# Products of 128 columns between longer ones, block sums from kept float32 tiles, and a new order, in a hybrid attention block on one core

## The chip, the core and the metric

The kernel runs on one core of a Trainium2 chip. The core has five engines with a queue each: TensorE (PE in the profile, with its weight loads listed apart as PEld), VectorE (DVE), ScalarE (ACT), GpSimd (POOL) and SyncE (SP), which here only issues DMAs. The metric is the time of one execution on the device, in microseconds (us). The kernel before took 420.25 us (median of three runs, 419.73 to 421.10).

## The reference, cut to what matters

One layer, float32, 512 tokens of 1024 channels. Two attention branches read the same normalised input and are merged by gates:

```python
h = rmsnorm(x, norm_g[l])
(q_lat, c_kv, k_rope, z_a, q_b, k_b, v_b, z_b,
 q_idx, k_idx, w_idx, gate_a, gate_b) = jnp.split(h @ w_in[l], cuts, axis=-1)
# branch a: 8 heads, latent q and k/v, shared rotary key, chunk-causal mask (chunks of 64)
y_a = mla_attention(q_nope, q_pe, k_nope, k_pe, v_a, pos).reshape(B, S, MLA_WIDTH)
y_a = y_a * jax.nn.silu(z_a)
# branch b: 8 heads; an indexer scores the keys, each query keeps its top 128, with a relative bias
y_b = dsa_attention(q_b, k_b, v_b, q_idx, k_idx, w_idx, rel_bias, pos, topk)
y_b = y_b * jax.nn.silu(z_b)
merged = (jax.nn.sigmoid(gate_a) * (y_a @ w_o_a[l])
          + jax.nn.sigmoid(gate_b) * (y_b @ w_o_b[l]))
x = x + merged @ w_out[l]
return rmsnorm(x, final_g)
```

Each branch computes, per head and per tile of 128 queries, `softmax(q @ k.T + mask or bias) @ v`. Because the mask is causal by chunks, query tile i (0 to 3) needs only the first 128 (i + 1) keys.

## The kernel before, in words

**Numbers.** Every float32 operand of a product is kept as two parts, `hi` (rounded for the fast format of TensorE) and `lo` (the rest). A product of two such operands is three products, hi hi, hi lo and lo hi, summed in a PSUM bank (`mm3`); where one operand needs no lo part it is two (`mm`). Every product is one weight load (a block of 128 columns) and one pass of up to 512 columns of the other operand.

**Tiles and room.** Most tiles of 128 x 512 come out of one pool (`slot`) of `NSLOT` = 73 tiles and four that are lent to the rotary tables and the rotary key first. A class of tiles can have a cap (`TCAP` = 5 for temporary tiles, `WCAP` = 8 for split weights). PSUM has 8 banks; the logits (`lg`) may hold two.

**Input.** `normed` makes the normalised input as eight tiles of 128 channels by 512 tokens: a float32 tile `tmp`, from it `hi` and `lo` (`hT[k]`), and gives `tmp` back.

**Projections.** Some are plain (`proj`: 24 products of 512 columns). Others come in pairs of column blocks and use a scheme with seven block products instead of eight (`seven`, called by `proj2` and `values2`, nine groups in all). The scheme needs sums and differences of blocks of the input, `hs`. `input_sums` makes them once `SUMS_AT` is done, which is head 5 of branch a: for each k it adds hi and lo of two input tiles to get float32 back, makes four differences and sums of 256 columns in place, and splits the two results into hi and lo, 16 tiles in all. In `seven`, a bank is taken out by ScalarE or VectorE between some block products, and the next ones that use it wait for that; the fourth product, which comes last, waits for the sum `c22`, an addition on VectorE.

**Heads of branch a** (`mla_head`). For each query tile i in `ORDER` (0, 1, 2, 3), one bank takes three products of 128 (i + 1) columns, lines 1664 to 1666. Then `soft` takes the row maximum on VectorE, the exponential on ScalarE, and normalises.

**Heads of branch b** (`dsa_head`). The mask tile i (16 rounds of top-8 on VectorE made it, `topk`) is copied into a bank by ScalarE, two products of 128 (i + 1) columns are added to it, and `soft` adds the bias on VectorE, then goes on as above.

**Values** (`attend`). The probabilities are turned on TensorE into key-major tiles (`turn`, line 481), split into hi and lo, and multiplied with the values: key tile 0 over 512 query columns, tile 1 over 384, tile 2 over 256, tile 3 over 128, two products each, one after the other in this order. Tile 3's probabilities lie in columns 128 to 256 of the third turned tile.

**Order.** The whole program is one list per engine, written out when the kernel is built. Each piece of work is a generator; a planner (`Flow.run`) keeps a rough clock for each engine and emits, over and over, the step that could start first. `prio` and a tiny random `nudge` (seeded by `DRAW`, and by `REDRAW` once the masks and the rotary key are made) break near ties. `FIRST` names 47 steps of the list at which the second or third candidate on the same engine is taken instead, and `PASSED` four loads of weights that are issued some DMAs later. So a change in any step changes the order of everything behind it. `QUEUE` is the order in which projections are fetched, split and multiplied.

Of the kernel before, what the change touches and what calls it, by code (L numbers as in the profile page):

```python
# [43 lines left out]
REDRAW = 324  # L44
# [121 lines left out]
class Flow:  # L166
# [9 lines left out]
    def __init__(self):  # L176
        self.free = {"PE": 0.6, "ACT": 0.6, "DVE": 0.6, "POOL": 0.6, "SP": 0.6}
        self.hw, self.dma, self.adma = 0.6, 0.0, 0.0
        self.pbias = -1.0
# [3 lines left out]

        self.draw = random.Random(DRAW)

    def spawn(self, gen, prio, nudge=None):
        t = Thread(gen, prio, self.draw.random() * NUDGE if nudge is None else nudge)
        self.threads.append(t)
        self.advance(t, None)
        return t  # L190
# [110 lines left out]
DRAW = 53  # L301
# [6 lines left out]
def tile_block(ctx: ExitStack, tc: tile.TileContext, a: dict, out: bass.AP, bias_dram: bass.AP):  # L308
# [159 lines left out]

    def mm3(ps, w, x, start, stop, more=False):

        return mm(ps, [(w[0], x[0]), (w[0], x[1]), (w[1], x[0])], start, stop, more)
# [102 lines left out]
    mask = [fixed(f"mask{i}", [P, P * (i + 1)]) for i in range(NT)]  # L574
# [68 lines left out]
    xt, eraw, xg, ewq, ewkv, eql, hT = {}, {}, {}, {}, {}, {}, {}  # L643
# [201 lines left out]
    def normed(k):  # L845
        yield Until(lambda: rbc and k in xg)
        tmp = yield slot("tmp", TCAP)
# [6 lines left out]
        put(tmp)  # L854
# [96 lines left out]
    def scores(i):  # L951
# [18 lines left out]
        if score_users[0] == 0:  # L970
            put(*qs.values(), *ks)
        flow.spawn(topk(i), PTOPK)
# [50 lines left out]
    sums_due = [SUMS_AT]  # L1023
# [66 lines left out]
    def input_sums():  # L1090

        yield Until(lambda: sums_due[0] in done)
# [455 lines left out]
    def attend(br, h, probs, ready, prio):  # L1548
# [29 lines left out]
        for kt, pt, src, dst in ((0, 0, slice(0, S), slice(0, S)), (1, 1, slice(P, S), slice(P, S)),  # L1578
                                 (2, 2, slice(256, S), slice(256, S)), (3, 2, slice(P, 256), slice(384, S))):
            hi, lo = turned[pt]  # L1580
            yield mm(ps[:, dst], [(v4[:, kt, :], hi[:, src]), (v4[:, kt, :], lo[:, src])], kt == 0, kt == 3)
            if kt != 2:
                put(hi, lo)
# [52 lines left out]
    def mla_head(h):  # L1636
# [7 lines left out]
        def soft(i, ps):  # L1644
# [3 lines left out]
                mx.tile[:, 1:2], ps.tile[:, :n], op=ALU.max, axis=AX.X, negate=True))], [mx], [ps])  # L1648
            den = yield from sums[i].at(i)
            yield act(probs[i], ps[:, :n], AF.Exp, bias=mx[:, 1:2], scale=1.0, accum=den)  # L1650
            put(ps, mx)
            yield from sums[i].normalise(i, probs[i])
            ready.add(i)

        for i in ORDER:
            nn = P * (i + 1)
            ps = yield bank("lg")

            def emit():
                o = ps.tile[:, :nn]  # L1660
                q0, q1 = qh.tile[:, TOK[i]], ql.tile[:, TOK[i]]
# [664 lines left out]
```

## Time and profile before

| What | Value |
|---|---|
| Runs of the kernel | 419.73, 420.25, 421.10 us |
| Span of the profiled execution | 417.4 us |
| Difference of the median from that span | 2.85 us |
| TensorE busy | 410.4 us, 2494 products, 2494 weight loads |
| VectorE, ScalarE, GpSimd busy | 372.8, 297.9, 125.7 us |
| Granted TensorE clock, 1.00 is full | 1.00 in every window up to 400 us |

The time of the profiled execution itself is not listed beside its span; its span is 2.85 us shorter than the median run, which also holds the program's start and end.

In a row of a group, the line number of the kernel comes first, then engine, operation, output and inputs by tile name (`ps` is a PSUM bank, `s_w` a split weight, `s_hs` a block sum, `s_ph` a turned probability), shapes, and the count; behind the bar, busy us and the mean ns of one, and then the idle time before them with what ended it. Rows of one tile give the shortest, middle and longest duration in ns, and the first and last start. In a row of the timeline the first number is the start and the second the duration, both in us; `x9` means that nine alike are merged, and brackets hold the idle time before with what ended it. A product is recorded from its entry into the array until its result is out, so neighbouring products overlap.

### The profile page before, as it was taken

The numbers are of one execution on the slowest core, as the hardware profiler recorded it, in microseconds if no ns is written. First come the engines' busy times: TensorE is split into PE (matmuls) and PEld (weight loads), VectorE is DVE, ScalarE is ACT, GpSimd is POOL, SyncE is SP. The second block draws the span as 40 slices with busy tenths as digits, with TensorE's granted clock in tenths as the row PEclk, the third lists the DMA queues.
The fourth block names the chain that finished last, engine by engine and source line by source line (L and its number), as shares of the span: only waits on it lengthen the run. The fifth ranks groups of instructions, "written<-read, shape, count | busy, mean of one in ns | idle before, by whom it ended". The sixth has DMA issues, their size and how long they took to land.

```text
span 417.4 us, 7522 instructions
## 1 busy us (share of the span) xinstructions
PE 410.4 (98%) x2494; PEld 370.5 (89%) x2494; DVE 372.8 (89%) x789; ACT 297.9 (71%) x688; POOL 125.7 (30%) x147
## 2 busy tenths in 40 slices
PE   8999999999999999999999999999999999999994
PEld 8999888888888888889999999999998888888883
DVE  4779889569999999999998999799889999999973
ACT  5776888575763846547649978998999975329753
POOL 0037769544464659610000410401001120021330
PEclk9999999999999999999999999999999999999999
DMA  7984135655256351553427336564249767377104
GB/s 266 359 291 143 51 93 190 182 172 136 100 134 188 97 166 40 139 140 110 143 53 204 111 127 175 143 150 149 93 113 296 249 184 240 107 263 264 50 26 176
DMA packets 30790, 65.90 MB, mean 158 GB/s; under 512 B 4792, under 2 KB 6472, under 8 KB 30752
## 3 DMA queue, kind: packets, MB, share of 16 engines
q1 hardware_dynamic: 28400, 61.79, 48.6%
q10 hardware_dynamic: 1584, 2.49, 1.7%
q0 software_dynamic: 768, 1.15, 0.9%
q8 instruction: 19, 0.31, 0.3%
q14 instruction: 19, 0.16, 0.1%
HBM read 50.49 MB, written 4.21 MB: 131 GB/s over the span
## 4 chain that ended last, share of the span: by engine, by line
PE 98%; DVE 0%; ACT 0%; DVEq 0%; issue 0%; ACTq 0%
PE ps L462 88%; PE ps L481 5%; PE ps L1665 1%; PE ps L1666 1%; PE ps L1664 1%; PE ps L957 1%; PE ps L611 1%; DVE s_rg L413 0%; ACT junk L366 0%; PE ps L1008 0%; DVEq L2322 0%; ACT sm L366 0%; DVE sm L2017 0%; DVE zeros L540 0%; DVE neghalf L540 0%
## 5 line engine op out<-in xcount | busy, mean ns | idle before, releaser
L462 PE MATMUL ps<-s_h,s_w 128*128 128x512 f32 (+1 forms) x672 | 135.8, 348 | 0.1
L462 PEld LDWEIGHTS ps<-s_h,s_w 128*128 128x128 f32 x672 | 106.8, 189 | 14.0 <-DVE s_pair L383 0.5
L357 ACT CAST s_w<-raw 128x512 fp32r<-128x512 f32 (+3 forms) x134 | 78.2, 595 | 16.1 <-DVE raw L383 12.1
L385 POOL TENSOR_TENSOR s_w<-raw,s_w 128x512 fp32r<-128x512 f32 (+2 forms) x42 | 52.1, 1253 | 61.5 <-ACT s_w L357 54.1
L383 DVE TENSOR_TENSOR s_w<-raw,s_w 128x512 fp32r<-128x512 f32 (+2 forms) x92 | 59.8, 663 | 9.7 <-ACT s_w L357 9.5
L462 PE MATMUL ps<-s_hs,s_w 128*128 128x256 f32 x384 | 51.9, 285 | 0.0
L462 PEld LDWEIGHTS ps<-s_hs,s_w 128*128 128x128 f32 x384 | 48.3, 191 | 0.1
L462 PE MATMUL ps<-s_ys,s_w 128*128 128x512 f32 x192 | 46.0, 392 | 0.0
L462 PEld LDWEIGHTS ps<-s_ys,s_w 128*128 128x128 f32 x192 | 35.7, 188 | 7.2
L462 PE MATMUL ps<-s_wo,s_mg 128*128 128x512 f32 (+1 forms) x156 | 33.7, 373 | 0.0
L462 PE MATMUL ps<-s_w,s_xg 128*128 128x328 f32 (+1 forms) x192 | 32.5, 323 | 0.0
L462 PEld LDWEIGHTS ps<-s_wo,s_mg 128*128 128x128 f32 x156 | 27.6, 188 | 5.2
L366 ACT ACTIVATE s_p<-s_p,sm 128x256 f32<-128x256 f32 (+3 forms) x58 | 31.0, 548 | 1.4 <-DVE sm L1748 1.3
L462 PEld LDWEIGHTS ps<-s_w,s_xg 128*128 128x128 f32 x192 | 31.4, 188 | 0.0
L357 ACT CAST s_ph<-ps 128x384 fp32r<-128x384 f32 (+1 forms) x48 | 23.6, 517 | 6.7 <-PE ps L481 5.7
L383 DVE TENSOR_TENSOR s_ph<-ps,s_ph 128x384 fp32r<-128x384 f32 (+1 forms) x48 | 27.2, 591 | 1.1 <-ACT s_ph L357 1.1
L366 ACT ACTIVATE s_p<-ps,sm 128x128 f32<-128x128 f32 (+3 forms) x32 | 16.8, 528 | 15.9 <-DVE sm L1647 15.8
L982 DVE MATCH_REPLACE8 mask<-sm,mask 128x384 f32<-128x384 f32 (+2 forms) x48 | 25.9, 542 | 0.0
L981 DVE MAX8 sm<-mask 128x8 f32<-128x384 f32 (+2 forms) x48 | 25.6, 548 | 0.1
L462 PE MATMUL ps<-s_ph,vv 128*128 128x512 f32 (+3 forms) x128 | 25.6, 319 | 0.0
L481 PE MATMUL ps<-ident,s_p 128*128 128x128 f32 x160 | 23.0, 273 | 0.0
L462 PEld LDWEIGHTS ps<-s_ph,vv 128*128 128x128 f32 x128 | 20.6, 189 | 2.0
(206 smaller groups left out, 783.4 us busy)
## 6 DMA issues: line engine op xcount, KB each, us to landing
raw<-w_out SPq DMA_DIRECT2D x18, 512.0 KB, 3.5
s_op<-s_op SPq DMA_DIRECT2D x36, 128.0 KB, 3.4
raw<-w_ga SPq DMA_DIRECT2D x8, 512.0 KB
raw<-w_gb SPq DMA_DIRECT2D x8, 512.0 KB, 3.6
raw<-w_o SPq DMA_DIRECT2D x16, 256.0 KB, 3.6
s_xn<-x SPq DMA_DIRECT2D x8, 256.0 KB, 5.2
bias_scratch<-s_sig ACTq DMA_DIRECT2D x8, 256.0 KB, 2.3
raw<-w_za SPq DMA_DIRECT2D x4, 512.0 KB, 4.5
```

The source lines that it names most:

```text
L357: nc.scalar.copy(dst.ap, src.ap)
L366: nc.scalar.activation(dst.ap, src.ap, func, **kw)
L383: opts.append(("DVE", 0.07 + 0.00104 * x.n, lambda: nc.vector.tensor_tensor(dst.ap, x.ap, y.ap, op=op)))
L385: opts.append(("POOL", 0.15 + 0.0021 * x.n, lambda: nc.gpsimd.tensor_tensor(dst.ap, x.ap, y.ap, op=op)))
L462: nc.tensor.matmul(ps.ap, l.ap, r.ap, start=start and i == 0, stop=stop and i == len(pairs) - 1, skip_group_check=more)
L481: nc.tensor.transpose(d.ap, s.ap, ident.tile)
L611: return lambda: nc.tensor.matmul(ps.tile[:, :n], z[:, :P], z[:, :n], start=True, stop=True)
L957: step = pe(0.005 + n / 2400, [ps.all], [qs[h].all, ks[0].all], lambda: nc.tensor.matmul(ps.tile[:, :n], qs[h].tile[:96, TOK[i]], ks[0].ti ...
L981: yield Step([("DVE", t, lambda: nc.vector.max(m8.tile, work.tile))], [m8], [work])
L982: yield Step([("DVE", t, lambda: nc.vector.match_replace(work.tile, m8.tile, work.tile, MARK))], [work], [m8])
L1664: nc.tensor.matmul(o, q0[0:100], k0[0:100], start=True, stop=False)
L1665: nc.tensor.matmul(o, q0[0:96], k1[0:96], start=False, stop=False)
```

## The change

Three things are changed, and the order is made anew.

1. Short products stand between longer ones. A helper `mixed` emits a list of products that may go to different views of one bank. In the logits, query tiles 2 and 0 share a bank (columns 128 to 512 and 0 to 128), and their products alternate, 384 and 128 columns; tiles 1 and 3 follow alone. In branch b the masks of tiles 0 and 2 lie in one tile of 512 columns and are copied into the shared bank at once. A shared bank is given back when both rows of `soft` are through with it. In `attend` the products of key tile 0 (512 columns) alternate with those of key tile 3 (128 columns) and come first; then come tiles 1 and 2.
2. `normed` keeps its float32 tile (class `hx`, no cap) and `input_sums` works in it, so the additions of hi and lo are gone. The sums start when head 1 of branch a is done.
3. `FIRST` and `PASSED` are empty, `DRAW` is 286 instead of 53 and `REDRAW` 186 instead of 324. `EARLY` and `MOVE` are new names with the old value and an empty table.

The number of products, the weights and the columns of each stay as they are.

```diff
@@ class Flow
-        self.pbias = -1.0
+        self.pbias = EARLY
...
@@
+    def mixed(parts, start, stop, more=False):
+        def emit():
+            for i, (o, l, r) in enumerate(parts):
+                nc.tensor.matmul(o.ap, l.ap, r.ap, start=start and i == 0, stop=stop and i == len(parts) - 1, skip_group_check=True)
...
@@
-    mask = [fixed(f"mask{i}", [P, P * (i + 1)]) for i in range(NT)]
+    two = const.tile([P, 4 * P], F32, name="masks")
+    mask = [Buf(two[:, :P], "mask0"), fixed("mask1", [P, 2 * P]), Buf(two[:, P:], "mask2"), fixed("mask3", [P, 4 * P])]
@@ def normed(k)
-        tmp = yield slot("tmp", TCAP)
+        tmp = yield slot("hx")
...
-        put(tmp)
+        hx[k] = tmp
@@ def input_sums()
-            f = []
-            for i in (k, k + 4):
-                t = yield slot("tmp", TCAP)
-                yield soon(tt(t.all.f, hT[i][0].all.f, hT[i][1].all.f, ALU.add, BOTH))
-                f.append(t)
+            yield Until(lambda: k in hx and k + 4 in hx)
+            f = [hx[k], hx[k + 4]]
@@ def attend
-        for kt, pt, src, dst in ((0, 0, slice(0, S), slice(0, S)), (1, 1, slice(P, S), slice(P, S)),
-                                 (2, 2, slice(256, S), slice(256, S)), (3, 2, slice(P, 256), slice(384, S))):
-            hi, lo = turned[pt]
-            yield mm(ps[:, dst], [(v4[:, kt, :], hi[:, src]), (v4[:, kt, :], lo[:, src])], kt == 0, kt == 3)
+        parts = []
+        for x in range(2):
+            for kt, pt, src, dst in ((0, 0, slice(0, S), slice(0, S)), (3, 2, slice(P, 256), slice(384, S))):
+                parts.append((ps[:, dst], v4[:, kt, :], turned[pt][x][:, src]))
+        yield mixed(parts, True, False)
+        put(*turned[0])
+        for kt, src in ((1, slice(P, S)), (2, slice(256, S))):
+            hi, lo = turned[kt]
+            yield mm(ps[:, src], [(v4[:, kt, :], hi[:, src]), (v4[:, kt, :], lo[:, src])], False, kt == 2, True)
@@ def mla_head
-        for i in ORDER:
+        for tiles in TILES:
             ps = yield bank("lg")
+            tiles = [(i, ps[:, c : c + P * (i + 1)]) for i, c in tiles]
+            yield mixed(logits(0, 0, 100, tiles) + logits(0, 1, 96, tiles) + logits(1, 0, 96, tiles), True, True)
@@ def dsa_head
-        for i in ORDER:
-            ps = yield bank("lg", (0, nn))
-            yield act(ps[:, :nn], mask[i].all)
-            yield mm(ps[:, :nn], [(qb[:, TOK[i]], kh[:, :nn]), (qb[:, TOK[i]], kl[:, :nn])], False, True, True)
+        for tiles in TILES:
+            ps = yield bank("lg", (0, width))
+            if len(tiles) > 1:
+                step = act(ps[:, :width], View(mask[0], two))
...
+            yield mixed([(o, qb[:, TOK[i]], k[:, : P * (i + 1)]) for k in (kh, kl) for i, o in tiles], False, True, True)
@@
-ORDER = [0,1,2,3]
+TILES = (((2, P), (0, 0)), ((1, 0),), ((3, 0),))
+EARLY = -1.0
+MOVE = {}
-FIRST = {
...
-}
-PASSED = {7: 2, 8: 2, 9: 2, 10: 6}
-SUMS_AT = ("a", 5)
+FIRST = {}
+PASSED = {}
+SUMS_AT = ("a", 1)
-REDRAW = 324
+REDRAW = 186
-DRAW = 53
+DRAW = 286
```

More of the change, by code (lines that the diff above doesn't have):

```diff
@@ L184, in __init__ @@
         self.draw = random.Random(DRAW)
+        self.born = {}
     def spawn(self, gen, prio, nudge=None):
-        t = Thread(gen, prio, self.draw.random() * NUDGE if nudge is None else nudge)
+        name = gen.__name__
+        n = self.born[name] = self.born.get(name, 0) + 1
+        drawn = self.draw.random() * NUDGE if nudge is None else nudge
+        t = Thread(gen, prio, MOVE.get((name, n), drawn))
         self.threads.append(t)
@@ L467, in mm @@
         return step
+    def mixed(parts, start, stop, more=False):
+        def emit():
+            for i, (o, l, r) in enumerate(parts):
+                nc.tensor.matmul(o.ap, l.ap, r.ap, start=start and i == 0, stop=stop and i == len(parts) - 1, skip_group_check=True)
+        t = sum(0.0133 + r.n / 2400 for _, _, r in parts)
+        step = pe(t, [o for o, _, _ in parts[:1]], [v for _, l, r in parts for v in (l, r)], emit, len(parts))
+        step.fills = [(o, start and i == 0) for i, (o, _, _) in enumerate(parts)]
+        return step
     def mm3(ps, w, x, start, stop, more=False):
@@ L971, in scores @@
             put(*qs.values(), *ks)
+            done.add("scored")
         flow.spawn(topk(i), PTOPK)
@@ L1642, in mla_head, with soft @@
         ready, sums = set(), sums_of_head()
-        def soft(i, ps):
+        def soft(i, ps, users):
             n = P * (i + 1)
@@ L1742, in dsa_head, with soft @@
         ready, biased, sums = set(), set(), sums_of_head()
[L1744 removed]
+        def soft(i, ps, users):
             n = P * (i + 1)
@@ L1748, in soft @@
             step = Step([("DVE", 0.1 + 0.00104 * n, lambda: nc.vector.tensor_tensor_reduce(
-                p.ap, ps.tile[:, :n], backward(bias.all.f[:, :n]).ap, op0=ALU.add, op1=ALU.min, scale=-1.0, scalar=-FILL,
-                accum_out=mx.tile[:, 1:2]))], [mx, p.buf], [ps, bias])
+                p.ap, ps.ap, backward(bias.all.f[:, :n]).ap, op0=ALU.add, op1=ALU.min, scale=-1.0, scalar=-FILL,
+                accum_out=mx.tile[:, 1:2]))], [mx, p.buf], [ps.buf, bias])
             step.count = 2
             yield step
-            put(ps)
+            users[0] -= 1
+            if not users[0]:
+                put(ps.buf)
             biased.add(i)
@@ L1762, in soft @@
             ready.add(i)
-        for i in ORDER:
-            nn = P * (i + 1)
-            ps = yield bank("lg", (0, nn))
-            yield act(ps[:, :nn], mask[i].all)
-            yield mm(ps[:, :nn], [(qb[:, TOK[i]], kh[:, :nn]), (qb[:, TOK[i]], kl[:, :nn])], False, True, True)
-            spawn(soft(i, ps), prio)
+        for tiles in TILES:
+            width = sum(P * (i + 1) for i, _ in tiles)
+            ps = yield bank("lg", (0, width))
+            if len(tiles) > 1:
+                step = act(ps[:, :width], View(mask[0], two))
+                step.ins.append(mask[2])
+                yield step
+            else:
+                yield act(ps[:, :width], mask[tiles[0][0]].all)
+            tiles = [(i, ps[:, c : c + P * (i + 1)]) for i, c in tiles]
+            yield mixed([(o, qb[:, TOK[i]], k[:, : P * (i + 1)]) for k in (kh, kl) for i, o in tiles], False, True, True)
+            users = [len(tiles)]
+            for i, o in tiles:
+                spawn(soft(i, o, users), prio)
         put(qb, kh, kl)
```

35 lines of the change are left out of this document (14 added, 21 removed), and 4 rows, old and new, of the table FIRST.

## The prediction

> **What bounds the kernel now.** I read the profile's page first: the shares of the engines and the chain that ended last. Then I read the windows by stage, the waits on the weight loads, and single products in order of time.
>
> ```profile
> span 417.4 us, 7522 instructions
> PE 410.4 (98%) x2494; PEld 370.5 (89%) x2494; DVE 372.8 (89%) x789; ACT 297.9 (71%) x688; POOL 125.7 (30%) x147
> ...
> PE 98%; DVE 0%; ACT 0%; DVEq 0%; issue 0%; ACTq 0%
> ```
>
> TensorE is busy for 410.4 of 417.4 us, and the chain lies on it for 98%. The windows (start:end, their length, then busy us and instructions of PE, PEld, DVE, ACT, POOL) say where the other 7.0 us are.
>
> ```profile
> 45.00:110.00 65.00, 65.00 (x350) 55.59 (x349) 53.26 (x102) 46.29 (x110) 38.82 (x49) 1.00 0.52 148
> 110.00:220.00 110.00, 110.00 (x652) 97.53 (x652) 109.09 (x258) 66.20 (x151) 44.49 (x50) 1.00 0.42 116
> 240.00:340.00 100.00, 99.92 (x733) 94.58 (x732) 91.73 (x191) 92.56 (x227) 13.43 (x10) 1.00 0.55 166
> 411.60:417.50 5.90, 0.00 (x0) 0.00 (x0) 1.04 (x3) 1.28 (x4) 0.00 (x0) 0.83 0.49 179
> ```
>
> Most of the idle time, 5.90 us, is the tail behind the last product; between 45 and 340 us TensorE has almost no hole. It has one partner near its limit in each stage: VectorE with 109.09 of 110 us before 220, ScalarE with 92.56 of 100 us after 240. A product is recorded as busy until its result is out, so a short wait does not show as idle on PE. It shows on the weight loads, in brackets with what ended it:
>
> ```profile
> 51.21 0.08 PEld L1008 LDWEIGHTS ps<-s_oh,rbs 64*8 64x8 f32 x1 [0.35 <-issue]
> ...
> 53.07 0.08 PEld L1008 LDWEIGHTS ps<-s_oh,rbs 64*8 64x8 f32 x1 [0.17 <-issue]
> ...
> 260.80 0.76 PEld L462 LDWEIGHTS ps<-s_h,s_w 128*128 128x128 f32 x6 [0.24 <-DVE s_pair L383]
> ...
> 299.81 0.77 PEld L462 LDWEIGHTS ps<-s_h,s_w 128*128 128x128 f32 x6 [0.24 <-DVE s_pair L383]
> ...
> 323.50 0.19 PEld L462 LDWEIGHTS ps<-s_op,qhi 128*128 128x128 f32 x1 [0.44 <-ACT ps L357]
> ```
>
> They add up to 0.35 + 0.17 + 0.24 + 0.24 + 0.44 = 1.44 us. So a better order alone has about 1.4 us to win; a worse one can lose much more. The rest must come from products that take less time each.
>
> **The change part by part.** *Products of 128 columns.* These are the groups that the change puts between longer ones, three in a logits tile of branch a, two in one of branch b, two in the attention values:
>
> ```profile
> L462 PE MATMUL ps<-s_ph,vv 128*128 128x128 f32 x32 | 5.3, 248 | 0.0
> ...
> L462 PE MATMUL ps<-s_op,qhi 128*128 128x128 f32 x16 | 2.7, 258 | 0.0
> ...
> L1666 PE MATMUL ps<-s_op,s_op 96*128 96x128 f32 x8 | 2.2, 276 | 0.0
> L1665 PE MATMUL ps<-s_op,qhi 96*128 96x128 f32 x8 | 2.2, 274 | 0.0
> L1664 PE MATMUL ps<-s_op,qhi 100*128 100x128 f32 x8 | 1.8, 226 | 0.0
> ```
>
> That is 32 + 16 + 24 = 72 products. What one costs is read from a run of three that stands between products of 512 columns, first the loads, then the products, by start time and duration:
>
> ```profile
> 83.24 0.19 PEld L462 LDWEIGHTS ps<-s_h,s_w 128*128 128x128 f32 x1
> 83.47 0.19 PEld L1664 LDWEIGHTS ps<-s_op,qhi 100*128 100x128 f32 x1
> 83.70 0.19 PEld L1665 LDWEIGHTS ps<-s_op,qhi 96*128 96x128 f32 x1
> 83.81 0.19 PEld L1666 LDWEIGHTS ps<-s_op,s_op 96*128 96x128 f32 x1
> 83.92 0.53 PEld L462 LDWEIGHTS ps<-s_h,s_w 128*128 128x128 f32 x3
> 84.50 0.19 PEld L1664 LDWEIGHTS ps<-s_op,qhi 100*128 100x128 f32 x1
> ```
>
> ```profile
> 83.23 0.62 PE L462 MATMUL ps<-s_h,s_w 128*128 128x512 f32 x2
> 83.70 0.23 PE L1664 MATMUL ps<-s_op,qhi 100*128 100x128 f32 x1
> 83.76 0.27 PE L1665 MATMUL ps<-s_op,qhi 96*128 96x128 f32 x1
> ```
>
> Each load starts when the product before it starts: 83.24 against 83.23, 83.70 against 83.70. The load for L1665 is not started at 83.47 or soon after, though the queue had nothing else to load until 83.70: weights are fetched one product ahead and no further. From load to load the run goes 83.70, 83.81, 83.92: 0.11 us for each product of 128 columns. The last of the three is followed by two products of 512 columns, which take (83.70 - 83.23) / 2 = 0.235 us each, up to the load at 84.50: 84.50 - 83.92 - 0.47 = 0.11 us again. The product itself could pass in 0.06 us (83.76 - 83.70: L1665 enters 0.06 us behind L1664, then waits for its weights). What holds it to 0.11 us is the load of the product that comes next, whatever length that has. The first of the run has a long product before it and the last a long one behind it, and both cost 0.11 us like the middle one. Alternated, each short product is first and last at once, and the long product behind it has its weights loaded in the shadow of the short one, as before. So I take 0 us for this part. The bounds: if the loads could run two ahead, 72 x (0.11 - 0.06) = 3.6 us less; nothing makes it dearer, since the count of products and loads stays, 2494 of each.
>
> [...]
>
> *Two logits tiles in one bank.* In branch b the mask copies of 128 and of 384 columns become one of 512.
>
> ```profile
> L357 ACT COPY ps<-mask 128x512 f32<-128x512 f32 x8 | 4.7, 583 | 0.6 <-DVE sm L1748 0.6
> L357 ACT COPY ps<-mask 128x384 f32<-128x384 f32 x8 | 3.8, 476 | 0.0
> ...
> L357 ACT COPY ps<-mask 128x128 f32<-128x128 f32 x8 | 2.1, 276 | 0.0
> ```
>
> ScalarE saves 8 x (0.476 + 0.276 - 0.583) = 1.35 us over the stage from 240 to 340, in which it is busy for 92.56 of 100 us. TensorE is busy for 99.92 us there, so nothing of it reaches the end unless it shortens the 0.44 us wait on ScalarE above. Against it: a head's first product now waits for a copy of 0.583 instead of 0.276 us, 0.31 us later, and the shared bank is free only when both softmax rows have read it. Products of other jobs cover that 0.31 us; without cover it is 8 x 0.31 = 2.5 us. I take 0.
>
> *Block sums from the kept tiles.* The eight additions that rebuilt the float32 input go; the subtractions, casts and low parts stay and come after head 1 of branch a instead of head 5.
>
> ```profile
> L383 DVE TENSOR_TENSOR s_y<-ps,s_tmp x16: 665/689/698, 103.8 to 344.6; 64x512 f32<-64x512 f32 x16
> L394 DVE SCALAR_TENSOR_TENSOR s_tmp<-s_x,normg,s_rbc x8: 740/745/1794, 33.7 to 42.7; 128x512 f32<-128x512 f32 x8
> ...
> L383 DVE TENSOR_TENSOR s_tmp<-s_h,s_h x6: 673/682/684, 172.6 to 186.4; 128x512 f32<-128x512 f32 x6
> ...
> L385 POOL TENSOR_TENSOR s_tmp<-s_h,s_h x2: 1294/1294/1294, 153.9 to 155.1; 128x512 f32<-128x512 f32 x2
> ...
> L357 ACT CAST s_hs<-s_tmp x8: 614/620/645, 159.2 to 190.1; 128x512 fp32r<-128x512 f32 x8
> L383 DVE TENSOR_TENSOR s_hs<-s_tmp,s_hs x7: 670/683/684, 170.6 to 191.3; 128x512 fp32r<-128x512 f32 x7
> ...
> L982 DVE MATCH_REPLACE8 mask<-sm,mask x48: 397/543/682, 100.5 to 215.0; 128x384 f32<-128x384 f32 x16, 128x512 f32<-128x512 f32 x16, 128x256 f32<-128x256 f32 x16
> ```
>
> VectorE loses 6 x 0.682 = 4.1 us and GpSimd 2 x 1.294 = 2.6 us. TensorE had 110.00 of 110 us there, so the gain is 0. The moved rest, 7 x 0.683 = 4.8 us of low parts on VectorE and 8 x 0.620 = 5.0 us of casts on ScalarE among it, falls into the same window; there the search for the top keys (48 replacements, 100.5 to 215.0) is VectorE's work of lowest rank and gives way. Without that cover up to 4.8 us of weight splits would come late; I take 0. The price is room, in a pool of 73 tiles and four lent ones: eight float32 tiles stay from 42.7 us on, when the last is written, and the sixteen sum tiles come up to 50 us earlier, since the first head of branch a ends at 103.8 us and the additions now begin at 153.9.
>
> *The new order.* The hand-written picks (47 steps, four held loads) go, and two new draws break the ties. No row shows what the picks were worth. From below it is the 1.44 us of waits; from above I take the third rival's price. As the pieces that it orders are the same, I take 0, nearer to the rows that show hardly a wait.
>
> **The sum.** 417.4 us of span and 0 + 0 + 0 + 0. The median of the runs, 420.25 us, is 2.85 us above the span of the profiled execution (start and end of the program), and that stays. **Forecast: no change, 420.2 us.** A measurement of this kernel tells about 0.3% from no change, 1.26 us.
>
> **The rivals.** *First, the alternation works*: the load of the long product's weights is hidden after all, because loads are spread over a long and a short product. For it: the first short product's own load is hidden already. Against it: a run of three would then take 0.06 + 0.11 + 0.11 us, and the rows show 0.11 each. Time: 420.2 - 3.6 = 416.6 us. [...]
>
> *Second, the order fills the waits*: the lighter VectorE and ScalarE and the early sums leave none of the 1.44 us. Time: 420.2 - 1.44 = 418.8 us. For it: three of the five waits end on those two engines. Against it: an order without the picks would have to be better everywhere at once.
>
> *Third, slower*: the last of the seven block products of a pair waits for VectorE's addition of the product two before it (the two waits of 0.24 us on s_pair). One product lies between as cover. The code has nine such groups, and their products stand in this row:
>
> ```profile
> L462 PE MATMUL ps<-s_hs,s_w x384: 274/283/365, 194.7 to 314.7; 128*128 128x256 f32 x192
> ```
>
> Seven of the nine show no such wait. In a new order VectorE, busy 91.73 of 100 us there, has other work queued ahead of that addition, or the room for split weights is taken by the sums and heads. Each group stops at three places of the code until ScalarE or VectorE has taken a bank. One wait of 0.24 us per group more is 9 x 0.24 = 2.2 us, 422.4 us; two are 4.3 us. It decides once the addition starts later than the covering product's length, twelve times at most 0.13 us (0.76 / 6 by the row at 260.80), 1.5 us. For it: this stage already has the most waits, and ScalarE has 7 us to spare in 100. Against it: ScalarE and VectorE both lose work.
>
> **How the numbers follow.** No change 0.38; alternation works 0.12, as the rows speak against it plainly; the waits filled 0.18; slower by hand-overs 0.32. The first and second rivals are faster by over 0.3%: 0.30. Slower is 0.32, same 0.38. The range reaches down to the alternation's 416.6 us and up to one and a half waits per group, 420.2 + 3.2 = 423.4 us, rounded outward to 416.5 and 423.6. The forecast's own range is 419.0 to 421.5.
>
> **What would show it.** Alternation: the load behind a 128-column product starts 0.11 us after that product's own start also between 384 or 512 columns (right), or 0.06 to 0.07 us (wrong, first rival). Bank sharing: the mask copies of 128 and 384 columns are gone and ScalarE is some 1.35 us lower. Sums: the group s_tmp<-s_h,s_h is gone and the casts to s_hs start before 130 us instead of at 159.2. Order: the bracketed waits on the weight loads add up to 1.4 us again; over 2.7 us makes the forecast wrong on the slow side. A tail that differs from 5.90 us by over 1 us would also break it.

## The result, and the profile after

The changed kernel takes 423.21 us (median; 422.65 to 424.00) against 420.07 us (419.73 to 421.10) of the kernel before: a ratio of 1.0075, with a 95% interval of 1.0056 to 1.0095. It is 3.1 us slower. The forecast was no change, 420.2 us; the time lies inside the range of 416.5 to 423.6 us.

The page of the profile after, the same lines as before (busy us, share of the span, instructions; then the chain that ended last, by engine):

```profile
span 421.2 us, 7537 instructions
...
PE 411.3 (98%) x2494; PEld 371.1 (88%) x2494; DVE 374.4 (89%) x785; ACT 293.9 (70%) x674; POOL 129.0 (31%) x149
...
PE 44%; DVE 6%; DMA 2%; ACT 2%; issue 1%; DVEq 0%; ACTq 0%
```

The span is 3.8 us longer than the 417.4 us of before, while TensorE works only 0.9 us more. Before, the chain lay on TensorE for 98%. Now it can be followed only from 185.79 us on (the shares add up to 55%), because there it leaves TensorE for VectorE. The windows by stage (start:end, length, then busy us and instructions of PE, PEld, DVE, ACT, POOL, then the granted clock) show which stage lost:

```profile
45.00:110.00 65.00, 64.54 (x348) 55.13 (x347) 55.14 (x104) 45.20 (x106) 39.14 (x48) 1.00 0.51 147
110.00:220.00 110.00, 108.05 (x622) 94.68 (x620) 105.73 (x258) 67.76 (x166) 47.31 (x54) 1.00 0.39 115
240.00:340.00 100.00, 99.47 (x742) 95.25 (x741) 89.56 (x190) 89.81 (x213) 14.53 (x10) 1.00 0.54 160
415.20:421.20 6.00, 0.10 (x1) 0.00 (x0) 1.32 (x4) 1.28 (x4) 0.00 (x0) 0.85 0.48 175
```

TensorE had 110.00 of 110 us before in the second window and has 108.05 now; the first and the third lost about 0.45 us each, and the tail is still 6 us. The waits on the weight loads, in brackets with what ended them, give the places. These are the five longest from 45 us on:

```profile
68.39 0.30 PEld L974 LDWEIGHTS ps<-s_qs,s_qs 96*128 96x128 f32 x2 [0.79 <-DVE s_tmp L387]
...
197.69 1.50 PEld L466 LDWEIGHTS ps<-s_hs,s_w 128*128 128x128 f32 x12 [0.58 <-ACT ps L361]
...
201.60 2.94 PEld L466 LDWEIGHTS ps<-s_hs,s_w 128*128 128x128 f32 x24 [0.97 <-ACT s_pair L361]
205.53 2.93 PEld L466 LDWEIGHTS ps<-s_h,s_w 128*128 128x128 f32 x24 [1.00 <-DVE s_pair L387]
...
327.18 0.30 PEld L478 LDWEIGHTS ps<-s_op,qhi 128*128 128x128 f32 x2 [0.73 <-ACT ps L361]
```

They sum to 0.79 + 0.58 + 0.97 + 1.00 + 0.73 = 4.07 us; four smaller ones, between 52 and 58 us, add 0.78: 4.85 us. Counted alike (every bracket from 45 us on), the kernel before has 1.75 us: the 1.44 of the prediction leaves out two short waits, 0.16 us at 51.45 and 0.15 us at 53.31. That is 3.1 of the 3.8 us. The three in the middle, 2.55 us, lie between 197 and 206 us, in the first of the nine groups of seven block products: its hand-overs from TensorE to ScalarE and VectorE are late. The last of the three, at 205.53, is the wait for the sum `c22`. What VectorE and ScalarE did meanwhile, in the timeline of that stretch (start, duration), a selection:

```profile
191.55 0.55 DVE L999 MAX8 sm<-masks 128x8 f32<-128x384 f32 x1
...
194.04 0.56 DVE L999 MAX8 sm<-masks 128x8 f32<-128x384 f32 x1
194.52 0.67 DVE L387 TENSOR_TENSOR raw<-raw 128x512 f32<-128x512 f32 x1
...
195.23 0.62 ACT L361 CAST s_w<-raw 128x512 fp32r<-128x512 f32 x1 [3.45 <-DVE raw L387]
...
196.75 0.62 ACT L361 CAST s_w<-raw 128x512 fp32r<-128x512 f32 x1 [0.40 <-ACT s_sig L370]
...
197.27 0.37 ACT L361 COPY ps<-ps 128x256 f32<-128x256 f32 x1
...
204.00 0.54 DVE L1000 MATCH_REPLACE8 masks<-sm,masks 128x384 f32<-128x384 f32 x1
204.46 0.68 DVE L387 TENSOR_TENSOR s_w<-s_wsum,s_w 128x512 fp32r<-128x512 f32 x1
205.06 0.42 DVE L387 TENSOR_TENSOR s_pair<-ps,s_pair 128x256 f32<-128x256 f32 x1
```

Read it from the bottom up. The addition that the last block product waits for (205.06, load at 205.53) stands in VectorE's list behind a round of the top-8 search. ScalarE's copy out of the first bank (197.27, load at 197.69) stands behind casts of split weights, and the first of these sat idle for 3.45 us until VectorE had made its operand (194.52), which itself stands behind two rounds of the search and the first step of a third. How much of VectorE's time the search has there, busy us (and instructions) on the mask tiles from 191.5 to 205.5 us, first in the changed kernel:

```profile
191.50:205.50 14.00, 8.34 (x22) 0.00 (x0) 0.00 (x0) 1.00 0.46 152
```

and in the kernel before:

```profile
191.50:205.50 14.00, 1.38 (x5) 0.00 (x0) 0.00 (x0) 1.00 0.42 132
```

8.34 against 1.38 us. The chain of waits from 190 to 212 us, by line, says the same; in the changed kernel TensorE has three tenths of it:

```profile
by line: DVE s_w L387 25.3%; PE ps L466 24.8%; DVE masks L1000 16.6%; DVE sm L999 14.6%; issue 7.3%; DVE raw L387 5.9%; PE ps L478 5.0%; DVE s_pair L387 1.6%; DVEq L387 0.1%
```

while in the kernel before it has all of it:

```profile
by line: PE ps L462 101.0%
```

The parts of the change that can be seen in rows of tiles did happen. The casts to the block sums and the last step of the mask tile of 384 columns, after (first and last start behind the comma):

```profile
L361 ACT CAST s_hs<-s_hx x8: 608/622/630, 118.2 to 154.6; 128x512 fp32r<-128x512 f32 x8
...
L406 DVE TENSOR_SCALAR masks<-masks x1: 350/350/350, 205.4 to 205.4; 128x384 f32<-128x384 f32 x1
```

The sums come 41 us earlier than before (118.2 against 159.2). The search ends at 205.4 us in place of 217.7: it runs earlier, at the cost of what stands beside it.

### The profile page after: what moved, and what is told of

Its sections match the earlier page's. It is cut to its first block, busy times and chain, and to the rows that moved or that the text cites. A ratio compares the mean times of both kernels' runs of the same rounds, so it can differ in the third digit from the quotient of the medians.

```text
span 421.2 us, 7537 instructions
## 1 busy us (share of the span) xinstructions
PE 411.3 (98%) x2494; PEld 371.1 (88%) x2494; DVE 374.4 (89%) x785; ACT 293.9 (70%) x674; POOL 129.0 (31%) x149
## 4 chain that ended last, share of the span: by engine, by line
PE 44%; DVE 6%; DMA 2%; ACT 2%; issue 1%; DVEq 0%; ACTq 0%
PE ps L466 40%; PE ps L478 3%; DVE s_w L387 2%; PE ps L497 2%; DMA raw<-w_zb 1%; DVE masks L1000 1%; DVE sm L999 1%; DMA raw<-w_out 1%; DVE raw L387 0%; ACT s_ys L370 0%; ACT s_w L361 0%; ACT s_p L370 0%; DVE s_y L387 0%; DVE s_wo L387 0%; ACT s_wo L361 0%
## 5 line engine op out<-in xcount | busy, mean ns | idle before, releaser
L387 DVE TENSOR_TENSOR s_w<-raw,s_w 128x512 fp32r<-128x512 f32 (+2 forms) x93 | 61.4, 673 | 8.6 <-ACT s_w L361 8.1
L466 PE MATMUL ps<-s_hs,s_w 128*128 128x256 f32 x384 | 50.6, 284 | 1.1 <-ACT s_pair L361 0.8
L466 PE MATMUL ps<-s_ys,s_w 128*128 128x512 f32 x192 | 44.9, 391 | 0.0
L389 POOL TENSOR_TENSOR s_w<-s_wsum,s_w 128x512 fp32r<-128x512 f32 x3 | 4.3, 1448 | 85.3 <-ACT s_w L361 85.3
L370 ACT ACTIVATE s_p<-s_p,sm 128x384 f32<-128x384 f32 (+3 forms) x52 | 28.3, 564 | 2.2 <-DVE sm L1762 1.8
L478 PE MATMUL ps<-s_op,qhi 128*128 128x256 f32 (+11 forms) x128 | 27.6, 319 | 0.5 <-ACT ps L361 0.5
L478 PEld LDWEIGHTS ps<-s_op,qhi 128*128 128x128 f32 (+2 forms) x128 | 20.9, 189 | 2.8 <-ACT ps L361 0.7
L361 ACT COPY s_tmp<-ps 64x512 f32<-64x512 f32 (+1 forms) x18 | 10.1, 561 | 15.2 <-PE ps L466 12.6
```

Source lines behind the costliest of these rows:

```text
L361: nc.scalar.copy(dst.ap, src.ap)
L370: nc.scalar.activation(dst.ap, src.ap, func, **kw)
L387: opts.append(("DVE", 0.07 + 0.00104 * x.n, lambda: nc.vector.tensor_tensor(dst.ap, x.ap, y.ap, op=op)))
L389: opts.append(("POOL", 0.15 + 0.0021 * x.n, lambda: nc.gpsimd.tensor_tensor(dst.ap, x.ap, y.ap, op=op)))
L466: nc.tensor.matmul(ps.ap, l.ap, r.ap, start=start and i == 0, stop=stop and i == len(pairs) - 1, skip_group_check=more)
L478: nc.tensor.matmul(o.ap, l.ap, r.ap, start=start and i == 0, stop=stop and i == len(parts) - 1, skip_group_check=True)
```

## The experiments

My theory after the result: the parts of the change are worth nothing, and the loss is the new order, at the three hand-overs of the first group, because VectorE's list there holds rounds of the search ahead of the group's work. Rivals: the alternation or the removed additions are worth something by themselves, and the order hides it; the lost picks are the loss; ScalarE or GpSimd is late there, not VectorE; the new structure (shared bank, early sums) cannot be ordered as well.

**Alternation undone, nothing else.** Same plan, but inside one step the short products stand behind the long ones.

```diff
     def mixed(parts, start, stop, more=False):
         def emit():
-            for i, (o, l, r) in enumerate(parts):
+            seen = [(o.first, o.n) for o, _, _ in parts]
+            for i, (o, l, r) in enumerate(sorted(parts, key=lambda p: seen.index((p[0].first, p[0].n)))):
```

> The changed kernel with the alternation alone undone: in the shared banks and in the attention values the short products follow the long ones in one run, on the same plan for all other engines. Theory (a product of 128 columns costs 0.11 us by the next weight load, wherever it stands): the same time as the changed kernel, 423.2 us within 0.5. Rival (alternation hides loads): up to 72 x 0.05 = 3.6 us slower, 426.8 us.

Measured: 422.73 us (422.61 to 423.71) beside 419.93 us of the kernel before; ratio 1.0067 (1.0051 to 1.0082). The alternated kernel has 1.0075, so alternation gains nothing. The loads for two shared logits banks, 12 in all, six of 384 and six of 128 columns, alternated in the changed kernel:

```profile
83.73 0.71 PEld L478 LDWEIGHTS ps<-s_op,qhi 100*128 100x128 f32 x4
84.43 0.30 PEld L478 LDWEIGHTS ps<-s_op,s_op 96*128 96x128 f32 x2
84.72 0.59 PEld L478 LDWEIGHTS ps<-s_op,qhi 100*128 100x128 f32 x4
85.29 0.30 PEld L478 LDWEIGHTS ps<-s_op,s_op 96*128 96x128 f32 x2
85.58 0.53 PEld L466 LDWEIGHTS ps<-s_h,s_w 128*128 128x128 f32 x3
```

and apart, in runs of three:

```profile
83.81 0.42 PEld L479 LDWEIGHTS ps<-s_op,qhi 100*128 100x128 f32 x2
...
84.69 0.19 PEld L479 LDWEIGHTS ps<-s_op,s_op 96*128 96x128 f32 x1
84.80 0.30 PEld L479 LDWEIGHTS ps<-s_op,qhi 100*128 100x128 f32 x2
...
85.67 0.30 PEld L466 LDWEIGHTS ps<-s_h,s_w 128*128 128x128 f32 x2
```

From the first of the 12 to the load behind them: 85.58 - 83.73 = 1.85 us alternated, 85.67 - 83.81 = 1.86 us apart. A short product inside a run takes 84.80 - 84.69 = 0.11 us; an alternated pair of 128 and 384 columns 84.72 - 84.43 = 0.29 us, which is 0.11 and the 0.18 us of a product of 384 columns (loads at 84.23 and 84.41 us, with the products apart).

**The picks alone, and the draws alone.** First the kernel before without its picks.

```diff
-FIRST = {
...
-PASSED = {7: 2, 8: 2, 9: 2, 10: 6}
+FIRST = {}
+PASSED = {}
```

> The kernel before with the hand-written picks and the held loads taken out, its own draws kept. Theory (the loss comes from an order without picks, and not from the new structure): bracketed waits of TensorE and its loads grow from 1.4 to 4 or more us and the time to 422.5 to 426 us. Rival (the early sums and kept tiles cause the loss): 420 to 421 us, hardly a wait more.

Measured: 421.25 us; ratio 1.0029 (1.0019 to 1.0039), less than the 422.5 us that I expected at the least. So the picks were worth 1.3 us on the old structure. Then the same kernel with the new draws on top.

```diff
-REDRAW = 324
+REDRAW = 186
...
-DRAW = 53
+DRAW = 286
```

> The kernel before without picks and with the changed kernel's two draws. Theory (order alone): 422 to 427 us, waits of 3 us or more, at places unlike the changed kernel's. Rival (structure): 420 to 421 us.

Measured: 433.92 us; ratio 1.0325 (1.0306 to 1.0344). Then the changed kernel with the old draws.

```diff
-REDRAW = 186
+REDRAW = 324
...
-DRAW = 286
+DRAW = 53
```

> The changed kernel with the two draws of the kernel before. Theory (order alone): any time from 421 to 427 us, with the waits at other places than 196 to 206 us. Rival (structure: sums early, tiles kept, loads late for the first group of block products): the first group waits again by 2 us or more, 423 us or more.

Measured: 435.81 us; ratio 1.0373 (1.0354 to 1.0392). Both lie above my ranges. Neither pair of draws suits the other structure; each was good only where it stood. Both crossed plans have one long hole near the end. In the waits of the changed kernel with the old draws (us in total, times, longest):

```profile
PEld ps L466 <- DVE s_wo L387: 6.8, 1, 6.8
```

So the other pair of draws costs 433.92 - 421.25 = 12.7 us on the old structure and 435.81 - 423.21 = 12.6 us on the new, four times the effect in question; a single redraw says nothing of a structure.

**Untuned draws on both.** Draws 7 and 7, without picks, on the kernel before and on the changed one, one execution each.

```diff
+REDRAW = 7
...
+DRAW = 7
```

> The kernel before without picks, both draws 7, a number chosen for nothing. Theory (draws that were not selected cost 5 us and more on either structure): 425 to 437 us, with a hole of several us in the output stage near 400 us. Rival (the structure before is the sounder one): under 424 us.

> The changed kernel with both draws 7. Theory (order alone): 425 to 437 us, within 8 us of the kernel before with draws 7 and no picks. Rival (the new structure costs time by itself): slower than that one by 3 us or more.

Measured: 442.83 us on the old structure, 426.51 us on the new. They differ by 16.3 us, twice what I allowed. That does not show the new structure to be better, since each is one plan out of many. The totals give no support to the rival that it can't be ordered as well; what stands in the first group does, as the table further down shows.

**The additions removed, on the old plan.** The planner reckons with the eight additions, but they are not emitted.

```diff
-                yield soon(tt(t.all.f, hT[i][0].all.f, hT[i][1].all.f, ALU.add, BOTH))
+                step = soon(tt(t.all.f, hT[i][0].all.f, hT[i][1].all.f, ALU.add, BOTH))
+                step.options = [(e, d, lambda: None) for e, d, _ in step.options]
+                yield step
...
+            hx, hy = (hT[i][0].all.f for i in (k, k + 4))
+            yield as_planned(tt(x[:, HI], hx[:, LO], hx[:, HI], ALU.subtract, BOTH), x, x)
...
```

> The kernel before on its own plan, every engine in the same order, with the eight additions of hi and lo not emitted; the block differences read the hi parts instead, so the lo part of the input is left out of the block sums. It shows what the removal is worth without a new order. Theory (the additions lie beside TensorE's work): 419.9 us within 0.5, VectorE busy for some 4 us less. Rival (VectorE's load decides the waits): 1 us or more faster, and the two waits of 0.24 us on s_pair gone.

Measured: 420.09 us beside 419.87 us; ratio 1.0006 (0.9997 to 1.0015). Its page:

```profile
PE 410.8 (98%) x2494; PEld 370.6 (89%) x2494; DVE 369.8 (88%) x783; ACT 297.9 (71%) x688; POOL 122.7 (29%) x145
```

VectorE and GpSimd are 3.0 us lower each (from 372.8 and 125.7), and the time stays. The removal is worth nothing on a fixed order.

**The hand-overs counted sooner.** The planner takes the hand-overs of the first group, then of all nine, as due 1.0 us sooner (`sooner` is `AHEAD` there and 0 elsewhere, in all seven hand-overs), so that they stand ahead in the lists of ScalarE and VectorE.

```diff
-        spawn(take("1", act(part(y), part(x))), 0)
+        spawn(take("1", act(part(y), part(x))), 0, flow.draw.random() * NUDGE - sooner)
...
+AHEAD = 1.0
```

> The changed kernel, in whose planner the seven steps that take the banks out in the first group of block products count as startable 1.0 us sooner, so that they go ahead of casts and subtractions of weights on ScalarE and VectorE; same draws; the plan is the same up to the first of these steps, and drawn anew after it. Theory (three hand-overs of that group, queued behind weight splits, cost 2.6 of the 3.1 us): the waits of 0.58, 0.97 and 1.00 us between 196 and 206 us are gone, and this group ends 2 to 2.6 us earlier; the total follows, 420.6 to 421.2 us, if the rest of the plan does not get worse. Rival (VectorE as a whole is late there, and any order waits): the group ends within 0.7 us of where it ended, its waits only moved to the weights s_w.

> The same 1.0 us for the hand-overs of all nine groups. Theory: no waits over 0.3 us on s_pair or on a bank copied for a group between 195 and 320 us, 420 to 421.5 us. Rival (hand-overs first make the weight splits and the heads late instead): 422.5 us or more, with waits on s_w, s_ph or the mask copies.

Measured: 436.14 us (ratio 1.0383, 1.0362 to 1.0403) and 430.86 us (1.0258, 1.0243 to 1.0273). The waits from 186 to 225 us with the first group sooner:

```profile
199.32 1.50 PEld L466 LDWEIGHTS ps<-s_hs,s_w 128*128 128x128 f32 x12 [1.16 <-ACT ps L361]
206.64 1.15 PEld L478 LDWEIGHTS ps<-s_op,qhi 128*128 128x128 f32 x8 [1.51 <-ACT ps L361]
```

The two waits on `s_pair` are gone, but the first hand-over waits for 1.16 instead of 0.58 us, and a mask copy behind the group for 1.51: 2.67 us in place of 2.55. Putting one piece ahead passes the lateness on to others. The rest of these plans is worse by itself, so their times say nothing of the group.

**The sums late again, and the tiles apart again.** Each in the changed kernel, with its own plan.

```diff
-SUMS_AT = ("a", 1)
+SUMS_AT = ("a", 5)
```

> The changed kernel with the block sums again started after head 5 of branch a; the float32 tiles stay kept longer; same draws, but the plan is another from about 112 us on. Theory (early sums are neutral, only the order counts): no wait ends on the block sums, and the time lies anywhere in the spread that the draws showed, 421 to 436 us, most likely slower than 423.2 since the two draws were not made for this plan. Rival (early sums push VectorE's work and cause the waits at 196 us): first group without waits, 420 to 421 us.

```diff
-TILES = (((2, P), (0, 0)), ((1, 0),), ((3, 0),))
+TILES = (((0, 0),), ((1, 0),), ((2, 0),), ((3, 0),))
```

> The changed kernel with one logits tile per bank, in the order 0, 1, 2, 3, as before the change (alternation only in the attention values); same draws, another plan from 84 us on. Theory (shared banks are neutral, the order counts): anywhere from 421 to 436 us, waits at other places, mask copies of 128 and 384 columns back and ScalarE 1.3 us busier. Rival (the shared bank makes heads wait, as in the 0.73 us behind the mask copy at 327 us): 419.5 to 421 us, no wait on a mask copy.

Measured: 427.29 us (1.0180, 1.0163 to 1.0197) and 433.89 us (1.0327, 1.0309 to 1.0345). With late sums the first group still waits:

```profile
200.79 2.93 PEld L466 LDWEIGHTS ps<-s_hs,s_w 128*128 128x128 f32 x24 [1.37 <-ACT s_pair L361]
204.89 2.93 PEld L466 LDWEIGHTS ps<-s_h,s_w 128*128 128x128 f32 x24 [1.17 <-DVE s_pair L387]
```

So the group is late without early sums too. With the tiles apart, the waits there are 0.74 and 0.40 us, but a hole of 6.36 us for the output weights opens at 400 us. Neither isolates its part: both measure another plan too. But the plans together show something that their times hide. The table has VectorE's time on the search (busy us on the mask tiles from 191.5 to 205.5 us) and the waits of the first group's loads:

| Plan | Search, us | Waits, us |
|---|---|---|
| kernel before | 1.38 | none |
| before, no picks | 1.81 | 0.76 |
| before, new draws | 1.17 | 0.33 |
| before, draws 7 | 6.22 | 1.56 |
| changed | 8.34 | 2.55 |
| changed, old draws | 8.24 | 1.57 |
| changed, draws 7 | 7.76 | 2.28 |
| changed, late sums | 8.19 | 2.54 |
| changed, tiles apart | 8.51 | 1.14 |

All five plans of the new structure in the table have the search there, whichever the draws; of the four on the old structure only one has. So it goes with the new structure more than with the draw. Late sums or tiles apart do not take it away; which part of the change brings it stays open.

**GpSimd kept out.** In the second group of weights the first two subtractions run on VectorE only; the planner may have lost time by giving one to GpSimd, at 1.3 us a piece.

```diff
+        how = ("DVE",) if len(pairs) == 2 else BOTH
-            yield soon(tt(t3, b22, b12, ALU.subtract, BOTH))
-            yield soon(tt(b12, b12, b11, ALU.subtract, BOTH))
+            yield soon(tt(t3, b22, b12, ALU.subtract, how))
+            yield soon(tt(b12, b12, b11, ALU.subtract, how))
```

> The changed kernel with the first two subtractions of weights of the second group of block products allowed on VectorE alone; same draws, same plan up to there (about 193 us), drawn anew behind. Theory (the first group waits because ScalarE's copy stands behind a cast that stands behind a subtraction that GpSimd delays: 1.29 us there, begun at 193.1 us): the subtraction on raw ends before 194.5 us instead of 195.2, and the wait of 0.58 us at 197.7 us is under 0.2 us. Rival (VectorE is late there whichever engine takes the first subtraction): the wait stays at 0.5 us or more. The total says little, as the plan behind is another one: 421 to 436 us.

Measured: 435.68 us (1.0380, 1.0361 to 1.0400). The subtraction that the cast waits for still stands behind the same rounds of the search, and the first hand-over still waits for 0.56 us. That piece on GpSimd is not the cause.

**The suspect taken away on the same plan.** The last seven rounds of the search for query tile 2 (those between 191 and 205 us) are planned but not emitted; then instead three casts ahead of the hand-overs on ScalarE read a table that is ready, so that VectorE does not hold ScalarE there; then both.

```diff
         for r in range(TOPK // 8):
...
+            kept = not (i == 2 and r >= 9)
-            yield Step([("DVE", t, lambda: nc.vector.max(m8.tile, work.tile))], [m8], [work])
+            yield Step([("DVE", t, lambda: kept and nc.vector.max(m8.tile, work.tile))], [m8], [work])
...
```

> The changed kernel on its own plan, every engine in the same order, with the last seven of the 16 top-8 rounds for query tile 2 left out (they stand on VectorE from 191.5 to 204.6 us); that tile's mask then keeps 72 keys instead of 128. Theory (VectorE's rounds stand ahead of the weight subtractions and of the addition that TensorE waits for): the waits of 0.58, 0.97 and 1.00 us between 196 and 206 us shrink to under 0.3 us together, and the time falls by 2 to 2.8 us, to 420.3 to 421.2 us. Rival (the casts on ScalarE alone hold up the copies): at most 1 us of the waits goes, 422.2 us or more.

```diff
+        free = {1: (4,), 2: (5, 6)}.get(len(pairs), ())
-            yield cast(hi.all, x)
+            step = cast(hi.all, x)
+            if n in free:
+                other = cast(hi.all, rbc[0].all.f)
+                step.options = [(e, d, emit) for (e, d, _), (_, _, emit) in zip(step.options, other.options)]
+            yield step
```

> The changed kernel on its own plan, with three casts of weights (product 4 of the first group, products 5 and 6 of the second) reading a table that is long ready instead of the differences that VectorE makes; so those weights are not the right ones, and ScalarE no longer waits for VectorE at these places. Theory (ScalarE's copies stand behind casts that wait): the waits of 0.58 and 0.97 us, which end on ScalarE, go; the one of 1.00 us, which ends on VectorE, stays; 1.2 to 1.7 us faster than the changed kernel, 421.4 to 422.0 us. Rival (ScalarE is late for another reason): under 0.5 us faster.

> Both edits at once, same plan: seven top-8 rounds of tile 2 left out and three casts reading a ready table. Theory (these are the waits, and nothing takes their place): no wait over 0.2 us between 190 and 210 us, 420.2 to 420.8 us, which leaves 0.3 to 0.9 us over the kernel before for the early wait at 68 us and the mask copy at 327 us. Rival (something else becomes late next): a new wait there, and under 1.5 us gained.

Measured beside 420.17 us of the kernel before: fewer rounds 420.66 us (ratio 1.0017, 0.9995 to 1.0038), free casts 424.16 us (1.0097, 1.0080 to 1.0114), both 420.75 us (1.0020, 1.0009 to 1.0032). With fewer rounds the whole stretch runs through; its loads from 190 to 210 us have no bracket:

```profile
196.38 2.95 PEld L466 LDWEIGHTS ps<-s_hs,s_w 128*128 128x128 f32 x24
199.26 1.51 PEld L466 LDWEIGHTS ps<-s_h,s_w 128*128 128x128 f32 x12
200.70 2.95 PEld L466 LDWEIGHTS ps<-s_hs,s_w 128*128 128x128 f32 x24
203.58 2.95 PEld L466 LDWEIGHTS ps<-s_h,s_w 128*128 128x128 f32 x24
```

With free casts, for which I had expected 421.4 to 422.0 us, ScalarE's two waits are gone, and VectorE's grows by as much:

```profile
199.53 2.95 PEld L466 LDWEIGHTS ps<-s_hs,s_w 128*128 128x128 f32 x24
205.16 4.11 PEld L466 LDWEIGHTS ps<-s_h,s_w 128*128 128x128 f32 x24 [2.69 <-DVE s_pair L387]
```

2.69 us in one wait against 2.55 in three. That the 24 loads behind it take 4.11 us instead of 2.95 is the clock, as the last section shows. The busy time from 192 to 207 us of PE, PEld, DVE, ACT and POOL, with fewer rounds:

```profile
192.00:207.00 15.00, 15.00 (x114) 14.46 (x113) 10.31 (x17) 9.60 (x20) 3.23 (x2) 1.00 0.55 176
```

and with free casts:

```profile
192.00:207.00 15.00, 12.52 (x95) 11.97 (x94) 14.63 (x33) 6.41 (x14) 2.04 (x2) 0.99 0.39 124
```

With free casts VectorE is full and TensorE has holes; with fewer rounds VectorE has 4.7 us free and TensorE has none. But a full VectorE alone makes no hole. The same window in the changed kernel and in the kernel before:

```profile
192.00:207.00 15.00, 13.05 (x95) 12.04 (x94) 14.69 (x35) 6.74 (x14) 2.40 (x2) 1.00 0.40 132
```

```profile
192.00:207.00 15.00, 15.00 (x122) 14.77 (x121) 14.82 (x30) 9.76 (x21) 0.00 (x0) 1.00 0.40 126
```

VectorE is as full before, 14.82 against 14.69 us, and TensorE has no hole. What differs is what stands ahead in VectorE's list. This shows the cause of these three waits: the seven rounds, which stand ahead of the group's work. Without them the ratio falls from 1.0075 to 1.0017, by 0.0058 x 420 = 2.4 us, about the sum of the three waits. The rival, that ScalarE's casts hold the hand-overs, falls: they only pass VectorE's lateness on. GpSimd falls too: with fewer rounds the subtraction runs at 192.35 us, before GpSimd's piece there has begun (192.66 us). On ScalarE the rows show ready work standing behind work that waits: in the changed kernel the bank of its step at 195.76 us (`s_sig`) is finished at 194.44 us, and ScalarE sits idle until 195.23 us, when the cast ahead of that step starts; with free casts the step starts at 194.09 us, and the idle time before it ends on TensorE. The copy at 197.27 us, whose bank is finished at 195.88 us, then stands behind a DMA issue (196.38 us, 0.33 us) and the cast at 196.75 us.

**The search counted later.** Can the planner be made to put the rounds behind? It reckons each round as starting 0.3, 0.6 or 1.5 us later than it could; nothing is left out.

```diff
-MOVE = {}
+MOVE = {("topk", n): 0.6 for n in (1, 2, 3)}
```

> The changed kernel, whose planner counts each top-8 round as startable 0.3 us later than it is, so that other work of VectorE goes first; same draws, another plan from about 97 us on, nothing left out. Theory (the rank of the rounds is the handle): first group's waits under 1 us, 420 to 422 us. Rival (every newly drawn plan loses elsewhere): 426 to 436 us.

> The same with 0.6 us. Theory: first group's waits under 0.7 us, 420 to 422 us. Rival: 426 to 436 us, whatever the first group does.

> The same with 1.5 us. Theory: first group's waits under 0.5 us, but the masks of branch b come later by several us; 420 to 424 us. Rival: 426 to 436 us, whatever the first group does.

Measured: 438.93 us (1.0473, 1.0434 to 1.0513), 439.60 us (1.0468, 1.0439 to 1.0496) and 479.39 us (1.1410, 1.1393 to 1.1427). All three are above my ranges. At 0.6 us the first group has no wait any more, with nothing left out: the search takes 6.2 us of VectorE from 191.5 to 205.5 us, and VectorE is busy for 14.11 us from 192 to 207, but the rounds stand behind the group's work. The last mask comes late, though (last start 270.6 us, row of the mask tiles), and with it branch b, whose first mask copy starts at 267.2 us instead of 205.8; TensorE then waits in its heads, 3.0 us for mask copies and 6.6 us for turned probabilities:

```profile
L406 DVE TENSOR_SCALAR mask<-mask x2: 276/351/426, 176.6 to 270.6; 128x256 f32<-128x256 f32 x1, 128x512 f32<-128x512 f32 x1
```

At 1.5 us the waits on their copies have become the largest item (us in total, times, longest):

```profile
PEld ps L478 <- ACT ps L361: 32.8, 7, 13.9
```

The search has to be done in time, and it has to give way in 14 us of the run; none of the three biases does both. No kernel of these experiments beats the kernel before.

## Why the prediction was wrong, step by step

**Alternation, 0 us: right.** What would show it was the load behind a short product 0.11 us later also between 384 columns; it is (0.29 us for a pair), and undoing the alternation on the same plan changes nothing. The first rival (416.6 us) falls: 1.85 against 1.86 us.

**Shared bank, 0 us: neither confirmed nor refuted.** The mask copies of 128 and 384 columns are gone. ScalarE fell by 4.0 us (297.9 to 293.9), not 1.35. The page has this row where the kernel before had 58 of the kind at 0.548 us:

```profile
L370 ACT ACTIVATE s_p<-s_p,sm 128x384 f32<-128x384 f32 (+3 forms) x52 | 28.3, 564 | 2.2 <-DVE sm L1762 1.8
```

Six normalisations of probabilities, 58 x 0.548 - 52 x 0.564 = 2.5 us, went to other engines in the new order, three each to VectorE and GpSimd. The later first product of a head, for which I had named 0.31 us and 8 x 0.31 without cover, may be part of the 0.73 us wait at 327.18 us, the only long one on a mask copy; that was not separated from the order.

**Block sums, 0 us: right for the removed additions, wrong in the cover that I named.** The additions are worth nothing on the old plan (ratio 1.0006). VectorE as a whole is not 4.1 us lower but 1.6 us higher in the changed kernel; which pieces the planner gave it in exchange was not followed row by row. I wrote that the search for the top keys is "VectorE's work of lowest rank and gives way". It does not: the list is fixed when the kernel is built, and in the new list the rounds stand ahead of the weights and of the sum `c22` (8.34 us of 14, against 1.38). I had priced the loss of this cover at up to 4.8 us and put it at nothing; about 2.4 us came.

**The new order: the step that failed, with that cover.** "As the pieces that it orders are the same, I take 0, nearer to the rows that show hardly a wait." Those rows showed one order, picked out of many; they are no evidence on the next one. The term measured +3.1 us. About 2.4 us of it lie in the first group (shown by taking the rounds away). The other 0.7 us is not traced: the waits at 68.39 and 327.18 us may be part of it, but the first of them lasted from 0.61 to 1.74 us in the four other runs on this plan. The picks alone, 1.3 us on the old structure, are a number that the prediction could not have from a row, though it could have had its sign; how much of the 3.1 us they are does not follow from it. That the loss is only a draw isn't shown either: by the table, the rounds come to stand there in all five plans of the new structure.

**The third rival was the right mechanism at nearly the right size** (hand-overs of the block products, 422.4 us; measured 423.2), with the condition that it named: VectorE has other work queued ahead of the addition. Its place was wrong, and that the size is near is luck. I spread it over nine groups, one wait of 0.24 us each, and gave VectorE's load from 240 to 340 us as the condition; it came in one group before 220 us, three hand-overs of 0.58 to 1.00 us, where the search and the weights of the next group meet. The waits over 2.7 us, which were to make the forecast wrong on the slow side, are 4.85. The second rival (418.8 us) fell with them; the tail kept its length.

**What stays open.** The shared bank and the early sums could be tried only with plans of their own, and the plans differ by up to 23 us on one structure (420 to 443 us). Which part of the change brings the search ahead of the first group isn't known. Whether a well picked order of the new structure would beat 420 us isn't settled.

## What to carry to other kernels

Where the order of every engine is written out at build time, a removed instruction is worth what it is worth on the same order, and that is measured by planning it and not emitting it; the new order is a term of its own, here 3 us for the change as made and 6 to 23 us in plans with draws that nobody picked. Look at what stands in the same place in several plans before calling a loss a draw. When TensorE waits, look past the engine that the bracket names to what that engine's list holds ahead: freeing ScalarE only moved the wait to VectorE, and it went only when the rounds were left out or stood behind the group's work. How full that engine was did not decide it (14.82 of 15 us without a hole). Products of 128 columns cost the 0.11 us of the next weight load here, alternated or in runs.

## What the runs showed of the hardware

Some holes of TensorE cost more than their length here. In the kernel before with the new draws, TensorE waits for 4.85 us near the end, up to 412.47 us; two windows behind it (PE busy us and products first, the granted clock third from the end):

```profile
413.00:417.60 4.60, 4.60 (x12) 3.57 (x11) 0.00 (x0) 0.00 (x0) 0.00 (x0) 0.50 0.00 0
417.60:420.00 2.40, 2.40 (x12) 1.94 (x12) 1.25 (x3) 1.52 (x4) 0.00 (x0) 1.00 0.00 0
```

The counts hold products that reach over an edge of the window. From start to start, a product of 512 columns takes 0.43 us at the granted clock of 0.50 and 0.23 us at 1.00, so the 4.60 us lose about 2.1 us more. Behind the hole of 6.8 us in the other crossed plan the clock is 0.54 for 4.6 us.

Shorter waits did it too, with a delay. With free casts the wait of 2.69 us ends at 205.16 us, and from 207 to 209 us the clock is 0.50: products of 256 columns start 0.21 us apart instead of 0.12. The window up to 207 us, with its 0.99, ends too early to show it. With draws 7 on the changed kernel the wait of 2.10 us ends at 202.69 us, and from 204 to 206 us the clock is 0.51. In these four runs waits of 2.10 to 6.8 us were followed by a clock of 0.50 to 0.54, while the waits of up to 1.00 us that this change made left it at 1.00 from 196 to 210 us; for waits between 1.00 and 2.10 us no clock is shown here. So the crossed plans lose part of their 12.6 us to the clock, and the changed kernel's first group does not.
